# Expert lists through a table in DRAM, and bias products with 128 rows, in a mixture-of-experts layer

## The chip, the cores and the metric

The kernel runs on one core of a Trainium2 chip. The metric is the device time of one execution in microseconds. Each kernel runs several times; the median of the runs is its time. A profile is taken of one further execution.

## The reference, cut to what matters

One layer of a diffusion backbone: a state-space branch and a windowed-attention branch, merged and normalised, and then the part that is changed here, a mixture of experts over 1024 tokens of width 1024 with 32 experts, four for each token:

```python
logits = xf @ w_router + b_router
top_v, top_i = lax.top_k(logits, 4)
gates = softmax(top_v)
# for the tokens of each expert e:
gu = xb @ w_gate_up[e] + b_gate_up[e]          # 1024 -> 2048
glu, lin = split(gu); glu = min(glu, 7); lin = clip(lin, -7, 7)
act = glu * sigmoid(1.702 * glu) * (lin + 1)
y[token] += gate * (act @ w_down[e] + b_down[e])  # 1024 -> 1024
```

The result goes through a residual and a last normalisation. All is float32.

## The kernel before

**Up to the experts.** The first part (up to about 1090 us) computes both branches, the normalisation and the router. It leaves in DRAM the modulated tokens `xm_d` and the accumulator `acc_d` (residual plus gated `b_down`). It also ranks the experts by how many tokens they have (`ranks`, line 1142) and leaves on chip `posr` (for each token and rank, the token's place in that expert's list, counted from 1, or 0), the one-hot columns `pick` of the ranks, and `info` (gate in three bfloat16 pieces, tile number, row number).

**The loop over the experts** (`moe`, line 1601). The experts are taken in `ORDER`: rank 0, 31, 1, 30, 2, 29 and so on, so one with many tokens and one with few in turn. Each rank has a fixed capacity (`CAPS`, from 256 down to 128). Those of even place in the order (ranks 0 to 14) are wide: two blocks, of 128 and of 128 down to 32 tokens; the others, and the last of even place, have one block of 128 and are called narrow. An expert is twelve steps: eight for gate and up, four for down. Each step multiplies with one weight chunk of 1 MB, loaded as two `raw` pieces of 0.5 MB by SyncE (`Weights.fetch`), split on chip into a high part by ScalarE (line 1491) and a low part by VectorE (line 1493), three steps ahead of its use. Each product is made three times (high-high, high-low, low-high; lines 1306 to 1309 for narrow experts, 1359 and 1360 for wide ones, where weights stand still and tokens stream).

**Lists.** While expert i computes, the list of expert i+2 is made. After step 2 `places` (line 1197) compares `posr` with a row of numbers, eight compares on VectorE. At step 5 `slots` multiplies these one-hots with `info`, eight small bfloat16 products per block on TensorE (line 1213) with one column per list place, and seven VectorE instructions per block (lines 1217 to 1226) turn the sums into row index `ri`, write index `wi` and gate `gt`. After step 8 `start` fetches the rows of `xm_d` by `ri` with an indirect DMA of GpSimd (line 1255). The rows are transposed on TensorE in steps 1, 6, 7 and 10 of the next expert (line 1277). After the down products the result is scaled by the gate and added into `acc_d` by an indirect DMA with accumulation (line 1442).

**Bias.** Wide experts add it on ScalarE. Narrow experts add it by a product (line 1320) of a selector `sel` of 64 rows, which `constants` makes from a tile of ones and `pick` (line 1264), with `bgu`, 64 rows that hold the high and low parts of all biases. There are four such products per narrow expert, after steps 1, 3, 5 and 7.

**Order.** In the loop the order on TensorE, VectorE and ScalarE is that of the program (`manual_schedule`); on GpSimd and SyncE a planner orders by when it expects operands to be ready. `weave` takes turns between several generators of instructions. `rest` (line 1722) treats experts that overflow their capacity; there are none in these inputs.

Of the kernel before, what the change touches and what calls it, by code (L numbers as in the profile page):

```python
# [8 lines left out]
F32 = mybir.dt.float32  # L9
F32R = mybir.dt.float32r  # L10
BF16 = mybir.dt.bfloat16
I32 = mybir.dt.int32
# [10 lines left out]
KT = 8  # L23
# [58 lines left out]
def body(tc, a, o):  # L82
    nc = tc.nc
    K = Ctx()
    es = ExitStack()
    with es:
        cst = es.enter_context(tc.tile_pool(name="cst", bufs=1))
        dram = es.enter_context(tc.tile_pool(name="dram", bufs=1, space=DRAM))
        K.ident = cst.tile([128, 128], F32, name="ident")
        nc.sync.dma_start(out=K.ident, in_=a["ident"])  # L90
        K.cols = cst.tile([128, 68], F32, name="cols")
        nc.sync.dma_start(out=K.cols, in_=a["cols"])
        K.xhat_d = dram.tile([S, D], F32, name="xhat_d")
        K.rows_d = dram.tile([4, D], F32, name="rows_d")
        K.xm_d = dram.tile([S, D], F32, name="xm_d")
        K.acc_d = dram.tile([S + 128, D], F32, name="acc_d")
        K.kv_d = dram.tile([NCTX + S, 256], F32, name="kv_d")
        K.q_d = dram.tile([S, 512], F32, name="q_d")
        K.gate_d = dram.tile([16, 128, S], F32, name="gate_d")
        K.o_d = dram.tile([4, 128, S], F32, name="o_d")  # L100
        K.ssm_d = dram.tile([8, 128, S], F32, name="ssm_d")
        K.z_d = dram.tile([S, 512], F32, name="z_d")
        K.win_d = dram.tile([4, 128, 8 * 2 * 128], F32, name="win_d")
        K.wout_d = dram.tile([4, 128, 2 * 8 * 128], F32, name="wout_d")
        K.m_d = dram.tile([4, 128, 8 * 128], F32, name="m_d")
        K.tab_d = dram.tile([64, 34], F32, name="tab_d")
        K.tabe_d = dram.tile([64, 1], I32, name="tabe_d")
        K.cst = cst
        K.dram = dram
        K.parts = {}  # L110
        K.mask = cst.tile([128, 8, 2, 32], BF16, name="mask")
        K.gts = cst.tile([128, 8, 32], F32, name="gts")
        K.b_cols = a["b_cols"]
        pre(tc, a, K, es)
        moe(tc, a, K)
        finish(tc, a, o, K)

# [954 lines left out]


CAPS = [256] * 3 + [240, 224, 208] + [192] * 4 + [160] * 5 + [128] * 17
BLOCKS = {256: (128, 128), 240: (128, 112), 224: (128, 96), 208: (128, 80), 192: (128, 64), 160: (128, 32), 128: (128,), 64: (64,)}
ORDER = [r for i in range(16) for r in (i, 31 - i)]
LIMIT = 7.0
SWIGLU = 1.702
TOP = float(np.float32(LIMIT / (1 + math.exp(-SWIGLU * LIMIT))))
# [2 lines left out]
def rank_consts(tc, a, K, tmp):  # L1082
    nc = tc.nc
    v = nc.vector
    late = K.late
    K.g2 = late.tile([128, D], F32, name="g2")
    nc.sync.dma_start(out=K.g2, in_=K.rows_d[3:4, :].to_broadcast([128, D]))
    K.route = late.tile([128, 67], F32, name="route")
# [10 lines left out]
    K.info = late.tile([128, 8, 32, 6], BF16, name="info")  # L1099
    K.iota = late.tile([128, 256], BF16, name="iota")  # L1100
    K.eid = late.tile([1, 32], I32, name="eid")
    K.pick = late.tile([64, 32], F32, name="pick")
    K.cnt = late.tile([64, 32], F32, name="cnt")
    K.rid = late.tile([64, 32], F32, name="rid")
    R = K.route
# [36 lines left out]
def ranks(tc, a, K):  # L1142
# [27 lines left out]
    v.tensor_scalar(K.eid, q[0:1, 0:32], -1.0, 31.0, ALU.mult, ALU.add)  # L1170
    yield
    v.tensor_copy(K.posr, p)
    v.tensor_copy(K.pick, K.pk.bitcast(F32))
    nc.scalar.activation(out=K.rid, in_=q[0:64, 0:32], func=ACTF.Copy)
    nc.scalar.activation(out=K.cnt, in_=q[0:64, 32:64], func=ACTF.Copy)

# [1 line left out]
def rank_gates(tc, K, pool):  # L1178

    nc = tc.nc  # L1180
    p = K.tp.tile([128, 512], F32, tag="tp", name="gr")[:, 0:256].rearrange("p (t e) -> p t e", t=8)
    for t in range(8):
        nc.tensor.matmul(p[:, t], lhsT=K.gT[:, t, :], rhs=K.pick[0:32], start=True, stop=True)
    gr = pool.tile([128, 8, 32], F32, bufs=1, name="gr")
    v = nc.vector
    v.tensor_copy(gr, p)
    for j in range(3):
        v.tensor_copy(K.info[:, :, :, j], gr)
        if j < 2:
            v.tensor_tensor(gr, gr, K.info[:, :, :, j], ALU.subtract)  # L1190
# [36 lines left out]
        yield out  # L1227


TURN = 5, 9  # L1230


class Expert:
# [24 lines left out]
    def constants(self):  # L1258
        nc, P, K = self.nc, self.P, self.K
        if self.wide:  # L1260
            nc.vector.tensor_scalar(self.bias[:, 8:16], self.bias[:, 8:16], 1.0, None, ALU.add)
        else:
            s = P.pk.tile([64, 256], F32R, tag="pk", name="pk")
            nc.vector.tensor_scalar(s, K.full, self.pick, None, ALU.mult)
            self.sel = s[:, 0:128] if self.n == 128 else s[:, 128:256]

    def lo(self, b):

# [63 lines left out]
    def act(self, q):  # L1332


        nc, P, nb = self.nc, self.P, self.n
        x = self.whole(self.gu, nb, ("hg", "hu")[q])[0:nb]
        t = P.tmp.tile([128, 512], F32, tag=("sg", "um")[q], name="t")[0:nb]
        if q == 0:
            nc.scalar.activation(out=t, in_=x, func=ACTF.Sigmoid, scale=SWIGLU)
# [244 lines left out]

def expert_consts(tc, a, K, late):
    nc = tc.nc
    K.bgu = late.tile([64, 2 * D], F32R, name="bgu")
    K.full = late.tile([64, 256], F32, name="full")
    nc.gpsimd.memset(K.full, 1.0)
    nc.gpsimd.memset(K.full[:, 192:256], 0.0)  # L1590
    br = K.wp.tile([128, KT, 256], F32, tag="raw", name="br").rearrange("p k n -> p (k n)")[0:64]
    for j in range(2):
        nc.sync.dma_start(out=br[j * 32:(j + 1) * 32], in_=a["b_gate_up"])
    nc.gpsimd.tensor_scalar(br[:, D:], br[:, D:], 1.0, 1.0, ALU.add, ALU.mult)
    for c in range(4):
        b, r = (x[:, c * 512:(c + 1) * 512] for x in (K.bgu, br))
        nc.scalar.activation(out=b, in_=r, func=ACTF.Copy)
        nc.gpsimd.tensor_tensor(b[32:64], r[32:64], b[32:64].bitcast(F32), ALU.subtract)


def moe(tc, a, K):
    nc = tc.nc
    es = ExitStack()
    with es:
# [4 lines left out]
        with ExitStack() as st:  # L1609
# [10 lines left out]
                return regs[r]  # L1620

            def place(i):
                if i < len(ORDER):
                    r = ORDER[i]
                    return places(tc, K, P.li, lambda t: K.posr[:, t, r:r + 1], CAPS[r])

            def lists(i, o, *steps):
                if i < len(ORDER):
                    r = ORDER[i]
                    return slots(tc, K, P.li, K.lg, o, lambda t: K.info[:, t, r, :], BLOCKS[CAPS[r]], *steps)  # L1630

            def start(i, ls):
                if i >= len(ORDER):
# [7 lines left out]
            with tc.manual_schedule(engines={mybir.EngineType.PE, mybir.EngineType.DVE, mybir.EngineType.Activation}):  # L1641
# [14 lines left out]
                weave(W.prepare())  # L1656
                cur.constants()
            prev = None
            with tc.manual_schedule(engines={mybir.EngineType.PE, mybir.EngineType.DVE, mybir.EngineType.Activation}):
                for i in range(len(ORDER)):  # L1660
                    xs = iter(nxt.x_parts()) if nxt else iter(())
                    for c in range(12):
# [1 line left out]
                            ls = next(lists(i + 2, oh) or iter(()), None)  # L1664
                        x = next(xs, None) if c in (1, 6, 7, 10) else None
                        cur.before(c)
                        weave(prev.store(1) if c == 0 and prev else None, cur.after(c), W.prepare(), x)
                        if c == 2:
                            oh = place(i + 2)
                        if c == 8:  # L1670
# [51 lines left out]
def rest(tc, a, K):  # L1722
    nc = tc.nc
    v = nc.vector
    with ExitStack() as es:
# [4 lines left out]
        with tc.For_i(0, count, 1) as i:  # L1730
# [15 lines left out]
                v.reduce_sum(f, w, axis=AX.X)  # L1746
                v.tensor_copy(inf[:, :, c], f)
            v.tensor_copy(inf[:, :, 3:6], K.info[:, :, 0, 3:6])
            pk = sm.tile([64, 1], F32, tag="pk", name="pk")
            v.tensor_tensor(pk, K.route[0:64, 65:66], row[0:64, 33:34], ALU.is_equal)  # L1750
            W = Weights(tc, a, P)
            W.add(eid)
            e = Expert(tc, K, P, (128,), pk, next(slots(tc, K, P.li, K.lg, places(tc, K, P.li, lambda t: pos[:, t:t + 1], 128),
# [461 lines left out]
def host(inputs):  # L2215
# [14 lines left out]
    w["ln_rows"] = np.stack([f("ln1_g")[0], f("ln1_b")[0], f("ln_in_g"), f("ln_in_b")])  # L2230
    w["ln2"] = np.stack([f("ln2_g")[0], f("ln2_b")[0]])
    w["route"] = route_table()
    w["sink"] = f("attn_sink")[0]
    i = np.arange(128)
    w["band"] = np.concatenate([np.where(i[None] >= i[:, None], 0.0, NEG), np.where(i[None] <= i[:, None], 0.0, NEG)],
# [24 lines left out]
```

## Time and profile before

| | us |
|---|---|
| median of three runs | 2746.44 (2744.35 to 2754.49) |
| the profiled execution | 2748.94 |
| its span, first to last instruction | 2746.8 |
| TensorE busy (matmuls) | 2513.2 (91%) |
| VectorE busy | 2190.4 (80%) |
| ScalarE busy | 1471.6 (54%) |
| GpSimd busy | 273.7 (10%) |

Busy times are of one profiled execution. Matmuls are pipelined and overlap in the records, so what one costs is read from its start to the next start. In the profile PE is TensorE's products, PEld its weight loads, DVE is VectorE, ACT ScalarE, POOL GpSimd, SP SyncE. PEclk is the granted TensorE clock as a share of the full one.

### The profile page before, as it was taken

The page shows a single profiled execution, that of the slowest core. Times are in us where ns is not written, and L with a number is a line of the kernel's source. Part 1 is how long each engine was busy: PE and PEld are TensorE (multiplying, and loading weights), DVE is VectorE, ACT ScalarE, POOL GpSimd, SP SyncE. Part 2 cuts the span into 40 slices and gives each one's busy share as a digit, 9 for nine tenths or more (in the row PEclk, how much of TensorE's full clock was granted, in tenths as well). Part 3 has the DMA queues.
Part 4 walks back from the last instruction along what each step waited for, and adds up shares of the span by engine and source line. Part 5 has one row for each costly group of instructions (what it writes and reads, how often), then busy time and mean ns, then how long its engine had stood idle before and what let it go on. Part 6 is the DMA issues. An engine that isn't in the chain of part 4 may idle for free. (4 is left out here: it accounts for less than half of the span.)

```text
span 2746.8 us, 41465 instructions
## 1 busy us (share of the span) xinstructions
PE 2513.2 (91%) x14030; PEld 2113.3 (77%) x14030; DVE 2190.4 (80%) x4354; ACT 1471.6 (54%) x2394; POOL 273.7 (10%) x173
## 2 busy tenths in 40 slices
PE   6799999889989886899999999999999999999990
PEld 1598887767778775788878878888988887888770
DVE  9735797348787757787987987988989899989995
ACT  0622112657766312555665665666666666666661
POOL 3300000000000004010100100111011011101113
PEclk8799999999999876899999999999999999999995
DMA  7434623644686782797987987998998999899984
GB/s 250 163 121 145 209 92 114 181 160 156 229 303 242 278 294 97 238 287 218 299 266 239 306 271 243 308 300 252 301 305 269 288 310 306 274 298 303 311 279 146
DMA packets 400937, 662.57 MB, mean 241 GB/s; under 512 B 36976, under 2 KB 203760, under 8 KB 393616
## 3 DMA queue, kind: packets, MB, share of 16 engines
q1 hardware_dynamic: 388416, 615.83, 67.0%
q0 software_dynamic: 11872, 42.47, 6.7%
q8 instruction: 112, 1.84, 0.3%
q10 hardware_dynamic: 432, 1.57, 0.2%
q14 instruction: 105, 0.86, 0.1%
HBM read 570.63 MB, written 89.15 MB: 240 GB/s over the span
## 5 line engine op out<-in xcount | busy, mean ns | idle before, releaser
L1493 DVE TENSOR_TENSOR wl<-raw,wh 128x1024 fp32r<-128x1024 f32 x768 | 921.6, 1220 | 162.4 <-ACT wh L1491 161.4
L1491 ACT ACTIVATE wh<-raw 128x1024 fp32r<-128x1024 f32 x768 | 789.6, 1052 | 244.0 <-PE dn L1309 88.7
L1359 PE MATMUL uw<-x,wh 128*128 128x320 f32 (+5 forms) x1920 | 578.3, 365 | 0.2 <-issue 0.2
L1360 PE MATMUL uw<-x,wl 128*128 128x192 f32 (+4 forms) x1920 | 500.2, 261 | 0.0
L1359 PEld LDWEIGHTS uw<-x,wh 128*128 128x128 f32 x1920 | 363.1, 189 | 23.5 <-issue 0.3
L1360 PEld LDWEIGHTS uw<-x,wl 128*128 128x128 f32 x1920 | 368.2, 192 | 0.5
L1306 PE MATMUL dn<-wh,a 128*128 128x512 f32 (+4 forms) x752 | 298.7, 397 | 0.0
L1307 PE MATMUL dn<-wl,a 128*128 128x512 f32 (+4 forms) x752 | 293.5, 390 | 0.0
L1309 PE MATMUL dn<-wh,a 128*128 128x512 f32 (+3 forms) x608 | 238.5, 392 | 0.6 <-DVE a L1286 0.6
L1306 PE MATMUL up<-wh,x 128*128 128x512 f32 x544 | 221.8, 408 | 0.0
L1442 POOL DMA_INDIRECT acc_d<-y,wi x47 | 118.9, 2531 | 959.5 <-DVE y L1440 815.8
L1309 PE MATMUL up<-wh,x 128*128 128x512 f32 x544 | 213.0, 392 | 0.0
L1307 PE MATMUL up<-wl,x 128*128 128x512 f32 x544 | 212.3, 390 | 0.0
L1371 ACT ACTIVATE t<-uw,bias 128x160 f32<-128x160 f32 (+5 forms) x240 | 98.6, 419 | 131.8 <-PE uw L1360 130.9
L1306 PEld LDWEIGHTS dn<-wh,a 128*128 128x128 f32 (+4 forms) x752 | 135.7, 180 | 37.8 <-issue 4.1
L1307 PEld LDWEIGHTS dn<-wl,a 128*128 128x128 f32 (+4 forms) x752 | 135.8, 181 | 33.8
L1309 PEld LDWEIGHTS dn<-wh,a 128*128 128x128 f32 (+3 forms) x608 | 112.8, 186 | 28.4 <-DVE a L1286 2.7
L1306 PEld LDWEIGHTS up<-wh,x 128*128 128x128 f32 x544 | 102.3, 188 | 27.4 <-issue 8.4
L1309 PEld LDWEIGHTS up<-wh,x 128*128 128x128 f32 x544 | 102.1, 188 | 22.4
L1307 PEld LDWEIGHTS up<-wl,x 128*128 128x128 f32 x544 | 102.4, 188 | 18.8
L51 PE MATMUL mm<-whi,uh 128*128 128x256 f32 x320 | 108.4, 339 | 4.4 <-DVE r L307 4.4
L52 PE MATMUL mm<-wlo,uh 128*128 128x256 f32 x320 | 107.7, 337 | 0.0
(529 smaller groups left out, 4970.7 us busy)
## 6 DMA issues: line engine op xcount, KB each, us to landing
raw<-w_gate_up SPq DMA_DIRECT2D x512, 512.0 KB
raw<-w_down SPq DMA_DIRECT2D x256, 512.0 KB
mw<-w_mod SPq DMA_DIRECT2D x64, 256.0 KB
raw<-w_in SPq DMA_DIRECT2D x13, 1024.0 KB
whi<-wo SPq DMA_DIRECT2D x10, 1024.0 KB
wlo<-wo SPq DMA_DIRECT2D x10, 1024.0 KB
raw<-w_mod SPq DMA_DIRECT2D x8, 1024.0 KB
gate_d<-gs SPq DMA_DIRECT2D x16, 512.0 KB
```

The lines of the kernel that those rows point to most:

```text
L51: nc.tensor.matmul(out, lhsT=lsel(lh, k), rhs=rsel(rh, k), start=start and k == 0, stop=False)
L52: nc.tensor.matmul(out, lhsT=lsel(lh, k), rhs=rsel(rl, k), start=False, stop=False)
L1306: nc.tensor.matmul(ps, lhsT=h, rhs=wh[:, k], start=st, stop=False)
L1307: nc.tensor.matmul(ps, lhsT=h, rhs=wl[:, k], start=False, stop=en and nb <= 64)
L1309: nc.tensor.matmul(ps, lhsT=X[:, k0 + k, lo:lo + nb], rhs=wh[:, k], start=False, stop=en)
L1359: nc.tensor.matmul(p[:, 0:2 * n], lhsT=wh[:, k, fs], rhs=self.x[:, k, 0:2 * n], start=k == 0, stop=False)
L1360: nc.tensor.matmul(p[:, 0:m], lhsT=wl[:, k, fs], rhs=self.x[:, k, 0:m], start=False, stop=k == KT - 1)
L1371: nc.scalar.activation(out=y[i], in_=self.uw[i][:, 1], func=ACTF.Identity, bias=self.bias[:, q * 8 + j0 + i:q * 8 + j0 + i + 1])
L1442: nc.gpsimd.indirect_dma_start(out=K.acc_d, out_offset=bass.IndirectOffsetOnAxis(ap=wi[0:nb], axis=0), in_=o[0:nb], in_offset=None, bounds ...
L1491: nc.scalar.activation(out=h, in_=r, func=ACTF.Copy)
L1493: nc.vector.tensor_tensor(l, r, h, ALU.subtract)
```

## The change

The lists of experts 1 to 6 of the order are made as before. For the 26 others a table `list_d` in DRAM has 1280 places for each rank, of 16 bytes: row index, write index, gate, nothing. It is first filled from an input with the values for empty places. A generator `spread`, two steps of it with each product step from the first expert on, finds for each token its four ranks and places with VectorE, and writes the four entries of each token by 32 indirect DMAs of GpSimd, each of 128 entries. `table` reads the list of one block by a DMA of SyncE. The selector of the bias products, `bgu` and `pick` get 128 rows, the upper 64 zero.

```diff
+        K.list_d = dram.tile([32 * LIST, 4], I32, name="list_d")
...
+LIST = 1280
+FIRST = 6
...
+    nc.sync.dma_start(out=K.list_d, in_=a["lists"])
     K.g2 = late.tile([128, D], F32, name="g2")
...
-    K.pick = late.tile([64, 32], F32, name="pick")
+    K.pick = late.tile([128, 32], F32, name="pick")
+    v.memset(K.pick[64:128], 0.0)
...
+    K.gr = pool.tile([128, 8, 32], F32, bufs=1, name="gr0")
+    nc.scalar.activation(out=K.gr, in_=p, func=ACTF.Copy)
...
+def spread(tc, K, pool):
+    base, key, mx, oh = t_("lb", [32]), t_("lk", [8, 32]), t_("lx", [8, 8]), t_("lo", [4, 32])
+    idx, pay = t_("li", [8, 4], I32), t_("lp", [8, 4, 4], I32)
+    v.tensor_scalar(base, K.route[:, 0:32], float(LIST), None, ALU.mult)
+    v.memset(pay, 0)
+    yield
+    v.scalar_tensor_tensor(key, K.posr, 0.0, base.unsqueeze(1).to_broadcast([128, 8, 32]), ALU.is_gt, ALU.mult)
+    yield
+    v.tensor_tensor(key, key, K.posr, ALU.add)
+    yield
+    for t in range(8):
+        v.max(out=mx[:, t], in_=key[:, t])
+        v.tensor_scalar(pay[:, t, :, 0:2], K.route[:, 64:65].unsqueeze(2).to_broadcast([128, 4, 2]), 128.0 * t, None, ALU.add)
+        yield
+    v.tensor_scalar(idx, mx[:, :, 0:4], -1.0, None, ALU.add)
+    for t in range(8):
+        yield
+        v.tensor_tensor(oh, key[:, t].unsqueeze(1).to_broadcast([128, 4, 32]), mx[:, t, 0:4].unsqueeze(2).to_broadcast([128, 4, 32]), ALU.is_equal)
+        v.tensor_tensor(oh, oh, K.gr[:, t].unsqueeze(1).to_broadcast([128, 4, 32]), ALU.mult)
+        yield
+        v.reduce_sum(pay[:, t, :, 2].bitcast(F32), oh, axis=AX.X)
+        for j in range(4):
+            nc.gpsimd.indirect_dma_start(out=K.list_d, out_offset=bass.IndirectOffsetOnAxis(ap=idx[:, t, j:j + 1], axis=0),
+                                         in_=pay[:, t, j], in_offset=None, bounds_check=32 * LIST - 1, oob_is_err=True)
+            yield
...
-            s = P.pk.tile([64, 256], F32R, tag="pk", name="pk")
-            nc.vector.tensor_scalar(s, K.full, self.pick, None, ALU.mult)
-            self.sel = s[:, 0:128] if self.n == 128 else s[:, 128:256]
+            self.sel = P.pk.tile([128, 128], F32R, tag="pk", name="pk")
+            nc.vector.tensor_scalar(self.sel, K.full, self.pick, None, ALU.mult)
...
-    K.bgu = late.tile([64, 2 * D], F32R, name="bgu")
-    K.full = late.tile([64, 256], F32, name="full")
+    K.bgu = late.tile([128, 2 * D], F32R, name="bgu")
+    K.full = late.tile([128, 128], F32, name="full")
...
+    nc.gpsimd.memset(br[64:128], 0.0)
...
             def place(i):
-                if i < len(ORDER):
+                if i < FIRST:
...
+            def table(r):
+                out = []
+                for b, nb in enumerate(BLOCKS[CAPS[r]]):
+                    x = P.li.tile([128, 4], I32, tag="tab%d" % b, name="tab")
+                    nc.sync.dma_start(out=x[0:nb], in_=K.list_d[r * LIST + b * 128:r * LIST + b * 128 + nb])
+                    out.append((x[:, 0:1], x[:, 1:2], x[:, 2:3].bitcast(F32)))
+                yield out
...
-                    return slots(tc, K, P.li, K.lg, o, lambda t: K.info[:, t, r, :], BLOCKS[CAPS[r]], *steps)
+                    return table(r) if i >= FIRST else slots(tc, K, P.li, K.lg, o, lambda t: K.info[:, t, r, :], BLOCKS[CAPS[r]], *steps)
...
+            to_lists = spread(tc, K, P.li)
...
-                        weave(prev.store(1) if c == 0 and prev else None, cur.after(c), W.prepare(), x)
+                        weave(prev.store(1) if c == 0 and prev else None, cur.after(c), W.prepare(), x, limit(to_lists, 2))
...
+    w["lists"] = np.tile(np.stack([np.zeros(128), S + np.arange(128), np.zeros(128), np.zeros(128)], axis=1), (32 * LIST // 128, 1)).astype(np.int32)
```

## Rows read from the trace of the kernel before

**Rows 1.** Stretches: start:end, length, busy us (instructions) by engine, PEclk, DMA share, GB/s.
```profile
1150.00:2680.00 1530.00, 1523.08 (x8300) 1285.92 (x8298) 1351.22 (x2446) 977.88 (x1386) 166.12 (x90) 1.00 0.89 282
```
**Rows 2.** Waits, 1150 to 2650 us: who, for whom: total us, times, longest.
```profile
ACT wh L1491 <- PE dn L1309: 88.7, 66, 3.5
...
ACT wh L1491 <- DMA raw<-w_down: 0.4, 1, 0.4
```
**Rows 3.** Timeline of TensorE, narrow expert: start, length, line, product.
```profile
2008.08 0.39 PE L1309 MATMUL up<-wh,x 128*128 128x512 f32 x1
2008.39 0.49 PE L1320 MATMUL up<-bgu,pk 64*128 64x512 f32 x1
2008.82 0.50 PE L1306 MATMUL up<-wh,x 128*128 128x512 f32 x1
2009.15 0.39 PE L1307 MATMUL up<-wl,x 128*128 128x512 f32 x1
2009.38 0.40 PE L1309 MATMUL up<-wh,x 128*128 128x512 f32 x1
```
**Rows 4.** Timeline of TensorE, the same expert, third bias product.
```profile
2021.75 0.49 PE L1320 MATMUL up<-bgu,pk 64*128 64x512 f32 x1
2022.17 0.71 PE L1277 MATMUL tp<-ident,x 128*128 128x128 f32 x4
```
**Rows 5.** Timeline of TensorE, the same expert, list products.
```profile
2017.76 0.35 PE L1213 MATMUL sl<-info,oh 128*128 128x6 bf16 x8
2018.41 0.66 PE L1277 MATMUL tp<-ident,t 128*128 128x128 f32 x4 [0.30 <-DVE t L1345]
```
**Rows 6.** Timeline of TensorE, list products in two wide experts.
```profile
1466.10 0.71 PE L1213 MATMUL sl<-info,oh 128*128 128x6 bf16 x16
1466.67 0.46 PE L1359 MATMUL uw<-x,wh 128*128 128x480 f32 x1
...
1869.64 1.93 PE L1213 MATMUL sl<-info,oh 128*128 128x6 bf16 x16
1871.50 0.44 PE L1359 MATMUL uw<-x,wh 128*128 128x384 f32 x1
```
**Rows 7.** Timeline of VectorE, the narrow expert of rows 3.
```profile
2013.38 1.39 DVE L1197 TENSOR_SCALAR oh<-iota,posr 128x128 bf16<-128x128 bf16 x8
...
2017.67 0.69 DVE L1345 SCALAR_TENSOR_TENSOR t<-t 128x512 f32<-128x512 f32 x1
...
2020.54 0.20 DVE L1217 TENSOR_REDUCE L<-sl 128x6 f32<-128x48 f32 x1
```
**Rows 8.** Stretches: second expert (narrow), third (wide), four late ones.
```profile
1185.00:1222.00 37.00, 36.57 (x172) 28.23 (x171) 34.92 (x50) 26.10 (x31) 6.50 (x3) 1.00 0.98 308
1222.00:1292.00 70.00, 70.00 (x386) 59.95 (x385) 54.80 (x106) 38.52 (x60) 4.42 (x3) 1.00 0.77 241
...
2400.00:2600.00 200.00, 199.06 (x1135) 167.38 (x1135) 184.25 (x339) 135.11 (x197) 22.65 (x12) 1.00 0.94 303
```
**Rows 9.** Timeline of GpSimd, ahead of the loop and in the second expert.
```profile
1088.72 1.28 POOL L1255 DMA_INDIRECT x<-xm_d,ri  x1 [0.82 <-DVE f L1222]
1090.03 1.27 POOL L1580 TENSOR_TENSOR h<-h,y 128x512 f32<-128x512 f32 x1
...
1188.64 2.34 POOL L1442 DMA_INDIRECT acc_d<-y,wi  x1 [34.93 <-DVE y L1440]
1198.20 3.08 POOL L1442 DMA_INDIRECT acc_d<-y,wi  x1 [7.21 <-DVE oh L1197]
1205.97 1.08 POOL L1255 DMA_INDIRECT x<-xm_d,ri  x1 [4.69 <-PE tp L1277]
```
**Rows 10.** Timeline of TensorE, third expert, first transposes of the fourth's rows.
```profile
1230.04 0.60 PE L1277 MATMUL tp<-ident,x 128*128 128x128 f32 x4
```
**Rows 11.** Tile x (fetched rows), 1150 to 2650 us: from issue to landing.
```profile
DMA to landing us min/median/max: 4.0/5.9/8.2
```
**Rows 12.** DMA queue of SyncE: packets, MB, share of 16 engines.
```profile
q1 hardware_dynamic: 388416, 615.83, 67.0%
```

More of the change, by code (lines that the diff above doesn't have):

```diff
@@ L1074 @@
 CAPS = [256] * 3 + [240, 224, 208] + [192] * 4 + [160] * 5 + [128] * 17
-BLOCKS = {256: (128, 128), 240: (128, 112), 224: (128, 96), 208: (128, 80), 192: (128, 64), 160: (128, 32), 128: (128,), 64: (64,)}
+BLOCKS = {256: (128, 128), 240: (128, 112), 224: (128, 96), 208: (128, 80), 192: (128, 64), 160: (128, 32), 128: (128,)}
 ORDER = [r for i in range(16) for r in (i, 31 - i)]
+LIST = 1280
+FIRST = 6
 LIMIT = 7.0
@@ L1172, in ranks @@
     v.tensor_copy(K.posr, p)
-    v.tensor_copy(K.pick, K.pk.bitcast(F32))
+    v.tensor_copy(K.pick[0:64], K.pk.bitcast(F32))
     nc.scalar.activation(out=K.rid, in_=q[0:64, 0:32], func=ACTF.Copy)
@@ L1227, in slots @@
         yield out
+def spread(tc, K, pool):
+    nc = tc.nc
+    v = nc.vector
+    t_ = lambda n, w, d=F32: pool.tile([128] + w, d, bufs=1, name=n)
+    base, key, mx, oh = t_("lb", [32]), t_("lk", [8, 32]), t_("lx", [8, 8]), t_("lo", [4, 32])
[22 more added lines that the diff above has]
+            yield
 TURN = 5, 9
@@ L1335, in act @@
         nc, P, nb = self.nc, self.P, self.n
-        x = self.whole(self.gu, nb, ("hg", "hu")[q])[0:nb]
+        x = self.gu[0:nb]
         t = P.tmp.tile([128, 512], F32, tag=("sg", "um")[q], name="t")[0:nb]
@@ L1586, in expert_consts @@
     nc = tc.nc
-    K.bgu = late.tile([64, 2 * D], F32R, name="bgu")
-    K.full = late.tile([64, 256], F32, name="full")
+    K.bgu = late.tile([128, 2 * D], F32R, name="bgu")
+    K.full = late.tile([128, 128], F32, name="full")
     nc.gpsimd.memset(K.full, 1.0)
-    nc.gpsimd.memset(K.full[:, 192:256], 0.0)
-    br = K.wp.tile([128, KT, 256], F32, tag="raw", name="br").rearrange("p k n -> p (k n)")[0:64]
+    br = K.wp.tile([128, KT, 256], F32, tag="raw", name="br").rearrange("p k n -> p (k n)")
+    nc.gpsimd.memset(br[64:128], 0.0)
     for j in range(2):
         nc.sync.dma_start(out=br[j * 32:(j + 1) * 32], in_=a["b_gate_up"])
-    nc.gpsimd.tensor_scalar(br[:, D:], br[:, D:], 1.0, 1.0, ALU.add, ALU.mult)
+    nc.gpsimd.tensor_scalar(br[0:64, D:], br[0:64, D:], 1.0, 1.0, ALU.add, ALU.mult)
     for c in range(4):
@@ L1748, in rest @@
             v.tensor_copy(inf[:, :, 3:6], K.info[:, :, 0, 3:6])
-            pk = sm.tile([64, 1], F32, tag="pk", name="pk")
-            v.tensor_tensor(pk, K.route[0:64, 65:66], row[0:64, 33:34], ALU.is_equal)
+            pk = sm.tile([128, 1], F32, tag="pk", name="pk")
+            v.memset(pk[64:128], 0.0)
+            v.tensor_tensor(pk[0:64], K.route[0:64, 65:66], row[0:64, 33:34], ALU.is_equal)
             W = Weights(tc, a, P)
```

## The prediction

> **What bounds the kernel now.** The stretches by engine come first. From 1150 to 2680 us, the whole loop over the 32 experts, TensorE is busy 1523.08 of 1530.00 us at a granted clock of 1.00 (the upper level, 2.4 GHz) [rows 1]. Then the waits of that stretch: ScalarE's splits of the weights wait for products to give their buffers back, and for a weight load once, 0.4 us [rows 2]. So transfers and splits run ahead of TensorE, and a microsecond taken out of TensorE's stream there is a microsecond of the run until something else comes late. The timeline of TensorE then shows what its non-weight instructions cost, read from start to start.
>
> **Bias products: 64 rows become 128.** A narrow expert (one block of 128 tokens) has four. At the row of one, the product before it starts at 2008.08, the bias product at 2008.39, the next products at 2008.82, 2009.15 and 2009.38 [rows 3]. Products of 128 rows follow each other by 0.23 us; the three steps around the bias product take 1.07 instead of 0.69, so 0.38 us go. After the change it has the form of its neighbours (128 rows, 512 columns, the same type), and I give it their 0.23. The third of the four is followed by transposes: 0.42 to them instead of 0.23, and the same 0.31 ahead of it, so 0.27 [rows 4]. Per expert 3 x 0.38 + 0.27 = 1.41; 17 narrow experts: 24.0 us. Bounds: nothing (the gaps stay) and 26.
>
> **Lists of experts 7 to 32 no longer made by matmuls.** These are 13 narrow experts and 13 of even place (12 with two blocks, one with one).
> - Narrow: the eight small products start at 2017.76, the transposes behind them at 2018.41: 0.65 us, of which 0.30 is a wait of TensorE for VectorE's t of line 1345 [rows 5]. This wait would stay if VectorE were no earlier, but the eight compares of line 1197 stand ahead of that t on VectorE, 1.39 us without a gap [rows 7], and they go too. So the t is ready at about 2018.36 - 1.3 = 2017.0, before 2017.76, and all 0.65 goes: 13 x 0.65 = 8.5 us. If only 0.35 goes each time: 4.5.
> - Wide: with a second block of 64 columns the sixteen products take from 1869.64 to 1871.50, 1.86 us; with 96 columns 1466.10 to 1466.67, 0.57 us [rows 6]. I take the first price, rounded to 1.8, for the lists with second blocks of 64 or 32 columns (four and five), and the second for those of 112, 96 and 80: 9 x 1.8 + 3 x 0.57 = 17.9 us; the last one, of one block, at nothing.
>
> Together 24.0 + 8.5 + 17.9 = 50.4 us off TensorE.
>
> VectorE loses per narrow list the 1.39 us and seven small instructions, per wide list more; it is not what ends, but in a narrow expert it is busy 34.92 of 37.00 us [rows 8], so it has to become lighter by as much as TensorE for the gain to hold. TensorE's narrow expert shrinks by 1.41 + 0.65 = 2.1 us, VectorE's by 1.39 plus the seven, of which the first takes 0.20 [rows 7] and the others are of one column: about 1.0 (at most 1.4). That is 2.4: it holds.
>
> **What is added.**
> - The spreading of the lists, two steps of its generator per product step, so from the first expert to the middle of the third. On VectorE 21 instructions of 8 to 256 columns, and three of 128 columns for each of the eight token tiles. One costs between the 0.17 us of a compare (1.39 / 8) and the 0.69 of a 512-column instruction [rows 7]; I take 0.2, nearest to the compare: 9 us in all, 2.4 of them (four tiles) in the second expert, the narrow one of 34.92 in 37.00. The weights are three steps ahead, 3 x 12 products at 0.23 = 8 us, which covers it; without that cover it is 2.4, with the upper price 8. I take 2.
> - 32 indirect writes of 128 x 16 bytes on GpSimd. They delay no engine by themselves; what stands behind them on that queue is the fetch of the rows of the fourth expert and the scatters. The fetch starts at 1205.97 and its rows are first used at 1230.04 [rows 9, 10]; landing takes 4.0 to 8.2 us, median 5.9 [rows 11]. So there are 18 us to lose. Each write also waits for the one before, since all write one table: two scatters into acc_d stand 9.56 us apart for that reason (1188.64 to 1198.20). One write plus wait lies between 1.08 us (the issue of a fetch) and 5.9 us (the landing of 512 KB; this is 2 KB); I take 3. Whether this costs depends on the order on GpSimd. The order there is not that of the program: a fetch of line 1255 at 1088.72 stands ahead of an add of line 1580 at 1090.03 which is emitted earlier [rows 9]. A fetch that is ready therefore gets between two writes, and I count nothing.
> - 38 table reads of 2 KB at most on SyncE's queue. Behind eight weight loads of 0.5 MB at 303 GB/s [rows 8] one lands at worst 13.8 us late; a fetch held from 1205.97 by that and landing in 5.9 comes at 1225.7, before 1230.04. Nothing.
> - The first filling of the table, 0.66 MB DRAM to DRAM, on SyncE's queue ahead of the loads for the output projection: read and written once at 303 GB/s 4.3 us, beside other work; I take 2. Bounds 0 and the rival below.
> - The clearing of rows (GpSimd, 64 x 2048 values at most) and one more copy of the gates (ScalarE): ahead of the loop, where both engines wait most of the time; nothing, at most 3 us.
>
> **Sum.** The profiled execution took 2748.94 us: 2748.94 - 50.4 + 2 + 2 = 2702.5. The median of the three runs is 2746.44, 2.5 lower: 2700 us. With 4.5 for the narrow lists the gain is 46, with 26 for the bias products 52; less 1 to 8 that is 2695 to 2708 when the mechanism is right.
>
> **Rivals.**
> 1. The transfers or VectorE take part of it back. For: in narrow stretches the DMA share is 0.98 (1185 to 1222) and from 2400 to 2600 it is 0.94 on average [rows 8]; a stretch 3% shorter needs 0.97. Against: 0.77 in the wide stretch between, and a single wait of 0.4 us for a load in 1530 us [rows 2, 8]. If the narrow experts after the sixth give back half of their 2.1 us, 13 x 1.05 = 14 us: 2714; if all, 2728.
> 2. The chain of writes blocks GpSimd once. If the order there is that of the program, twelve writes stand between the second scatter (its issue ends 1201.28) and the fetch of the fourth expert. At 3 us each the fetch starts at 1237.3, lands at 1243.2, and TensorE stands 13 us: 2713. With 5.9 us each: 1272.1, 1278.0, 48 us: 2748, no change. Against: the reordering in [rows 9]. The Trainium skill, "DMA: Bandwidth & Descriptors", section "Anatomy of one DMA — SWDGE (gpsimd) path", speaks against the change here: a small transfer from GpSimd's queue costs about 2.0 us whatever its size, mostly the confirmation of the write, worst with HBM as target. With it one write plus issue would be 3.1 us and the stop an estimated 14 us; no row here shows so small a transfer.
> 3. Slower than before: the filling is cut as the table is shaped, into 40960 pieces of 16 bytes. By the queue's row a packet takes 0.670 x 16 x 2746.8 / 388416 = 0.076 us [rows 12]; with that 40960 x 0.076 / 16 = 195 us in which all later loads of SyncE's queue stand behind it, ahead of the router: 2700 + up to 195 = 2895. It decides from 46 us on, that is 0.018 us per piece. Against: both sides are contiguous, so nothing asks for pieces.
> 4. The change doesn't do what it says: the bias products keep their gaps. Then 24 us stay: 2724. Against: the neighbours in [rows 3] differ from it in nothing but the row count.
>
> **Chances.** Forecast 0.66, rival 1 0.13, rival 2 0.10, rival 3 0.05, rival 4 0.03, other slower ways 0.03. Likeliest 2700. The range 2688 to 2730 holds the forecast, rival 1, rival 4 and the cheaper half of rival 2. A measurement of this kernel can tell about 0.5% from no change, so faster means below 2732.7: 0.66 + 0.13 + 0.03 and half of rival 2, and some of the rest: 0.85; within 0.5%: 0.08; slower: 0.07.
>
> **What would show it.** After the change: starts around line 1320's product 0.23 apart; line 1213 with 304 products fewer; no wait of TensorE's transposes for line 1345's t from the sixth expert on; the loop over the experts about 48 us shorter, TensorE still over 99% busy in it; the time before 1150 within 3 us of before. It is wrong if TensorE has a gap of over 5 us in the third expert (rival 2), if ScalarE's splits wait for loads in narrow experts (rival 1), or if the loop starts later by tens of microseconds (rival 3).

## The result, and the profile after

The changed kernel is slower: 2763.91 us (median of 20 runs, 2754.81 to 2778.30) against 2749.23 for the kernel before in 20 runs beside it; ratio 1.0057, 95% interval 1.0046 to 1.0069. The forecast was 2700. The profiled execution has a span of 2761.9 us.

Lines moved: 1213 is now 1220, 1255 is 1294, 1277 is 1315, 1306 to 1309 are 1344 to 1347, 1320 is 1358, 1345 is 1383, 1442 is 1480, 1474 is 1512, 1491 is 1529, 1493 is 1531. New are 1264 (the writes into the table) and 1669 (the reads).

First the loop by stretches, as in [rows 1] (busy us of each engine, granted clock, DMA share, GB/s):

```profile
1150.00:2680.00 1530.00, 1479.27 (x7936) 1273.27 (x7935) 1283.31 (x1954) 978.19 (x1382) 199.22 (x121) 0.98 0.89 282
```

TensorE was busy 1523.08 of these 1530 us before. Now 51 us are idle, and the granted clock is 0.98 where it was 1.00. Over the whole loop, from the first gate-and-up product to the last down product, TensorE is busy 1530.93 of 1588.88 us; before it was 1560.12 of 1572.92. So its work did shrink, but it waits. The waits from 1150 to 2650 us (who, for whom: total us, times, longest) say for what, and answer to [rows 2]:

```profile
POOL list_d L1264 <- DMA list_d<-lp,li: 75.6, 24, 5.9
...
ACT wh L1529 <- DMA raw<-w_gate_up: 49.8, 47, 20.0
...
ACT wh L1529 <- DMA raw<-w_down: 46.7, 64, 2.2
...
PE tp L1315 <- DVE t L1383: 29.9, 12, 4.2
...
PE tp L1315 <- DMA x<-xm_d,ri: 13.3, 1, 13.3
```

ScalarE waited for weight loads 0.4 us in the loop before, 96.5 now. The waits of SyncE, which issues these loads, in the same stretch:

```profile
SPq L1669 <- DMA acc_d<-y,tab: 126.0, 19, 9.0
...
SPq L1669 <- DMA list_d<-lp,li: 32.7, 1, 32.7
```

Both lines are table reads: they stand until something else has landed, and the weight loads stand behind them.

Where in the loop this falls is seen by cutting it into experts, from each first gate-and-up product on TensorE to the next expert's (worked out from the starts, us; the experts are counted in the order in which they are taken; means where several are named). Each ratio is to executions of the kernel before taken beside that kernel, with medians from 2747.64 to 2749.23 us; it is taken over all executions and need not be the quotient of two medians.

| kernel | time, us | ratio to before, 95% interval | 3 | 4 | 8, 10, 12 | 14 to 22, narrow | 24, 26, 28 |
|---|---|---|---|---|---|---|---|
| before | 2749.23 | | 68.2 | 39.2 | 39.2 | 39.5 | 39.4 |
| after | 2763.91 | 1.0057 (1.0046 to 1.0069) | 82.6 | 52.1 | 36.9 | 43.6 | 39.1 |
| bias_only | 2742.23 | 0.9979 (0.9967 to 0.9990) | 68.2 | 39.0 | 38.9 | 39.1 | 39.0 |
| lists_only | 2762.00 | 1.0056 (1.0036 to 1.0076) | 82.7 | 51.2 | 38.4 | 41.7 | 38.9 |
| slow_writes | 2729.47 | 0.9932 (0.9912 to 0.9952) | 68.2 | 40.3 | 37.1 | 42.3 | 39.1 |
| many_bufs | 2734.67 | 0.9932 (0.9903 to 0.9961) | 82.2 | 58.9 | 37.3 | 37.4 | 37.3 |
| first8 | 2754.24 | 1.0028 (1.0017 to 1.0038) | 79.9 | 52.4 | 37.0 | 42.1 | 39.2 |
| act_reads | 2724.98 | 0.9906 (0.9883 to 0.9930) | 78.8 | 52.0 | 36.9 | 37.3 | 37.3 |
| slow_many | 2705.94 | 0.9840 (0.9826 to 0.9853) | 68.2 | 40.3 | 37.1 | 37.3 | 37.3 |
| slow_act | 2702.04 | 0.9831 (0.9817 to 0.9844) | 68.2 | 40.3 | 37.0 | 37.3 | 37.3 |
| slow_many64 | 2724.24 | 0.9914 (0.9899 to 0.9929) | 68.2 | 40.3 | 38.4 | 38.7 | 38.7 |

In after, the narrow experts 8 to 12 gain 2.3 us each, a little more than forecast, and the wide ones from 7 on 0.3 to 3.5. The third and fourth lose 27 together, the narrow ones 14 to 22 lose 4 each where they should have gained 2. Before the loop nothing is lost (first product at 1103.7 us, 1105.7 before).

**The third expert.** The timeline of GpSimd in after (start, length, line, operation, idle time before it and what ended it), answering to [rows 9]:

```profile
1204.85 1.57 POOL L1480 DMA_INDIRECT acc_d<-y,wi  x1 [5.18 <-DVE gt L1232]
1206.73 2.01 POOL L1264 DMA_INDIRECT list_d<-lp,li  x1 [0.30 <-issue]
1214.60 0.99 POOL L1264 DMA_INDIRECT list_d<-lp,li  x1 [5.86 <-DMA list_d<-lp,li]
1221.02 1.94 POOL L1264 DMA_INDIRECT list_d<-lp,li  x1 [5.43 <-DMA list_d<-lp,li]
1228.43 1.92 POOL L1264 DMA_INDIRECT list_d<-lp,li  x1 [5.48 <-DVE wl L1531]
1235.17 0.98 POOL L1264 DMA_INDIRECT list_d<-lp,li  x1 [4.82 <-DMA list_d<-lp,li]
1238.92 0.98 POOL L1264 DMA_INDIRECT list_d<-lp,li  x1 [2.77 <-DMA list_d<-lp,li]
1240.21 1.06 POOL L1294 DMA_INDIRECT x<-xm_d,ri  x1 [0.30 <-issue]
```

Six writes stand between the second scatter and the fetch of the fourth expert's rows, 6.4 us from one to the next ((1238.92 - 1206.73) / 5), because four of these five times the write waits for the landing of the one before, and once for VectorE. The fetch starts at 1240.21, 34 us later than before. TensorE then, where [rows 10] had a start at 1230.04 without a wait:

```profile
1245.21 1.09 PE L1315 MATMUL tp<-ident,x 128*128 128x128 f32 x4 [13.25 <-DMA x<-xm_d,ri]
```

These four transposes take 1.09 us against 0.60: from 1245.00 to 1248.00 us, right after the stop, the granted clock is 0.50 (the lower of its two levels, 1.2 GHz). TensorE's busy time in the third expert is 69.39 us, 1.22 more than before, and that is what the expert loses beyond the 13.25.

**The fourth expert.** SyncE's timeline in after:

```profile
1273.85 1.90 SPq L1512 DMA_DIRECT2D raw<-w_gate_up  x2
1308.53 1.87 SPq L1669 DMA_DIRECT2D tab<-list_d  x4
1310.65 1.03 SPq L1512 DMA_DIRECT2D raw<-w_gate_up  x2
```

The first table read was put ahead of the weight loads and stands 32.7 us, until the last write (issued at 1304.7) has landed. From 1260 to 1310 us the DMA share is 0.41. ScalarE's next split and, under it, TensorE's product behind it:

```profile
1314.71 1.06 ACT L1529 ACTIVATE wh<-raw 128x1024 fp32r<-128x1024 f32 x1 [20.03 <-DMA raw<-w_gate_up]
```

```profile
1315.82 0.50 PE L1344 MATMUL up<-wh,x 128*128 128x512 f32 x1 [3.70 <-ACT wh L1529]
```

TensorE is idle 10.0 us in this expert, 5.4 of them from 1330 to 1340 us, where it waits for VectorE, which is busy 19.8 us from 1320 to 1340. The granted clock over the expert is 0.90.

**The narrow experts from the fourteenth on.** SyncE and, under it, GpSimd in the sixteenth:

```profile
1915.49 10.69 SPq L1512 DMA_DIRECT2D raw<-w_gate_up  x5
1933.20 0.34 SPq L1669 DMA_DIRECT2D tab<-list_d  x1
1933.79 5.69 SPq L1512 DMA_DIRECT2D raw<-w_down  x8
```

```profile
1924.34 3.55 POOL L1480 DMA_INDIRECT acc_d<-y,tab  x1 [29.07 <-DVE y L1478]
1933.93 1.84 POOL L1480 DMA_INDIRECT acc_d<-y,tab  x1 [6.03 <-DVE wl L1531]
```

A table tile has four buffers. The read that fills one again waits until the scatter that used its old content as write indices has landed, and the planner has put that read ahead of eight loads of `w_down`. What TensorE makes of it in the sixteenth, and then the stretches of 1952 to 1958 us, of the whole sixteenth and of the twenty-fourth expert:

```profile
1952.69 1.09 PE L1315 MATMUL tp<-ident,t 128*128 128x128 f32 x4 [3.52 <-DVE t L1383]
```

```profile
1952.00:1958.00 6.00, 5.31 (x15) 4.38 (x16) 5.43 (x6) 2.83 (x4) 0.00 (x0) 0.50 1.10 349
1921.11:1964.74 43.63, 40.11 (x173) 32.19 (x172) 36.71 (x42) 28.59 (x33) 7.70 (x4) 0.92 0.95 292
2310.26:2349.17 38.91, 37.48 (x174) 30.20 (x173) 36.20 (x42) 28.54 (x33) 8.37 (x4) 1.00 0.92 288
```

TensorE stands 3.52 us, because VectorE, which makes the low parts from the splits, is late, and then runs at a granted clock of 0.50 for some microseconds. In each of the narrow experts 14 to 22 it is idle 3.0 to 4.2 us, the clock over the expert is 0.92, and its busy time is 2.7 to 2.9 us longer than in slow_act (below), where the clock is 1.00. In 24, 26 and 28 it is idle 1.4 to 2.0 us and the clock stays at 1.00. SyncE stands about as long in both groups, 6.8 to 7.7 us in each expert. So nearly half of what the experts 14 to 22 lose is slower products and not waiting.

Two rules of the Trainium skill bear on this, both on the page "DMA: Bandwidth & Descriptors", section "Anatomy of one DMA — SWDGE (gpsimd) path". It says that a wait for a semaphore is served by the engine that issues the DMA, ahead of the issue, and not by the DMA engines. The trace agrees: the waits stand on SyncE (126.0 and 32.7 us) and on GpSimd (75.6 us), and issues behind them are late. The Trainium skill also gives, in the same section, about 2.0 us for a small transfer, mostly until the write is confirmed. From issue to landing the writes of 2 KB take, by the view of the table's tile in after:

```profile
DMA to landing us min/median/max: 2.1/4.3/7.6
```

The minimum is near the figure of the Trainium skill, and the median, with weight loads running beside the writes, is twice it; the measurement decides.

### The profile page after: what moved, and what is told of

Same layout as the page of the kernel before. It is cut to its first block, busy times and chain, and to the rows that moved or that the text cites. A ratio compares the mean times of both kernels' runs of the same rounds, so it can differ in the third digit from the quotient of the medians.

```text
span 2761.9 us, 40561 instructions
## 1 busy us (share of the span) xinstructions
PE 2480.9 (90%) x13726; PEld 2109.9 (76%) x13726; DVE 2137.9 (77%) x3926; ACT 1476.5 (53%) x2395; POOL 309.2 (11%) x205
## 3 DMA queue, kind: packets, MB, share of 16 engines
q1 hardware_dynamic: 393088, 616.55, 66.5%
## 5 line engine op out<-in xcount | busy, mean ns | idle before, releaser
L1531 DVE TENSOR_TENSOR wl<-raw,wh 128x1024 fp32r<-128x1024 f32 x768 | 924.5, 1220 | 239.1 <-ACT wh L1529 234.9
L1529 ACT ACTIVATE wh<-raw 128x1024 fp32r<-128x1024 f32 x768 | 795.1, 1053 | 311.3 <-PE dn L1347 78.8
L1480 POOL DMA_INDIRECT acc_d<-y,tab x38 | 88.1, 2319 | 598.6 <-DVE y L1478 488.8
L1294 POOL DMA_INDIRECT x<-xm_d,tab x38 | 51.0, 1343 | 549.2 <-PE tp L1315 500.9
```

Source lines behind the costliest of these rows:

```text
L1294: nc.gpsimd.indirect_dma_start(out=x[0:nb], out_offset=None, in_=K.xm_d, bounds_check=S - 1, oob_is_err=True, in_offset=bass.IndirectOffse ...
L1480: nc.gpsimd.indirect_dma_start(out=K.acc_d, out_offset=bass.IndirectOffsetOnAxis(ap=wi[0:nb], axis=0), in_=o[0:nb], in_offset=None, bounds ...
L1529: nc.scalar.activation(out=h, in_=r, func=ACTF.Copy)
L1531: nc.vector.tensor_tensor(l, r, h, ALU.subtract)
```

## The experiments

**bias_only and lists_only: the two halves of the change.** bias_only is the kernel before with the 128-row parts of the diff alone. lists_only is after with

```diff
-            nc.tensor.matmul(p, lhsT=self.sel, rhs=K.bgu[:, c0:c0 + 512], start=False, stop=True)
+            nc.tensor.matmul(p, lhsT=self.sel[0:64], rhs=K.bgu[0:64, c0:c0 + 512], start=False, stop=True)
```

Expected of bias_only:

> Theory (the bias products are worth what the rows of before say, 1.41 us in each of 17 narrow experts, and the loss of the change lies in the lists alone): the kernel before with the 128-row bias products takes 24 us less than before, about 2725 us; each narrow expert shortens from 39.4 to about 38.0 us, the wide ones stay within 0.3. Rival A (the shorter narrow experts of after come from the lists that are no longer made, and the gap around the bias product is not worth 0.38): under 8 us less, 2741 or more. Rival B (shorter narrow experts run into the transfers by themselves, which is what lengthened the experts 14 to 22 of after): from the fourteenth expert on the narrow ones do not shorten, ScalarE's splits wait for loads, and the total gains at most 10 us.

Measured: 2742.23, 6.8 us below before. The narrow experts up to the thirtieth gain 0.0 to 0.5 us each, not 1.41; only the last two, during which no list is made any more, gain 1.3 and 1.4. The total is in rival A's range and the experts are as rival B has them, but the reason is neither's. The stretches of the eighteenth expert, in before, bias_only and slow_act (below), in this order:

```profile
2002.38:2041.83 39.45, 39.15 (x182) 30.20 (x180) 38.47 (x57) 28.16 (x33) 6.09 (x3) 1.00 1.00 318
```

```profile
1999.30:2038.47 39.17, 37.75 (x181) 30.46 (x180) 38.46 (x57) 28.15 (x33) 6.36 (x3) 1.00 1.01 316
```

```profile
1985.00:2022.35 37.35, 37.34 (x173) 30.27 (x172) 36.38 (x41) 28.46 (x33) 7.84 (x3) 1.00 1.00 318
```

The busy time of TensorE (second number) falls by 1.40 in bias_only, which is the forecast's 1.41. VectorE (fourth) is busy 38.46 of 39.17 and holds the expert. TensorE in bias_only, where [rows 5] had 0.30:

```profile
2013.86 0.35 PE L1214 MATMUL sl<-info,oh 128*128 128x6 bf16 x8
2015.32 0.66 PE L1277 MATMUL tp<-ident,t 128*128 128x128 f32 x4 [1.10 <-DVE t L1345]
```

In bias_only ScalarE waits only 0.3 us for weight loads from 1500 to 2650 us: the transfers are not what holds it.

Expected of lists_only:

> The kernel after with the bias products cut back to 64 rows (rows 0 to 63 of the same tiles). Theory (the losses are the chain of GpSimd's writes and SyncE's standing table reads, whatever the bias products take): the fourth expert's rows are late as after (third expert about 82, fourth about 52 us), the narrow experts 14 to 22 still take 43 to 45 us, and the total is 10 to 24 us above after, 2774 to 2788; not the whole 24, because a longer narrow expert hides more of SyncE's standing. Rival (the losses arise only because the bias products make the narrow experts too short for the transfers): narrow experts 14 to 22 take under 41 us, and the total is at or below after, 2764 or less.

Measured: 2762.00, where after has 2763.91: the whole gain of the 128 rows is lost in after. The third and fourth lose as in after; narrow experts 8 to 12 take 38.4, 1.5 more than in after; but 14 to 22 take 41.7 (40.2 to 44.0) against 43.6, so what the bias products give there, SyncE's standing takes, and more. The theory has the experts and misses the total; the rival has the total, and its bound of 41 us fails for two of the five. In these five experts TensorE is idle 17.5 us together in after and 11.0 in lists_only, and the granted clock, 0.92 in all five of after, is 0.96 in two and 1.00 in three of lists_only. The shorter experts wait longer, and more of their products run at the lower clock.

**slow_writes: the chain of writes stretched.** After with

```diff
-FIRST = 6
+FIRST = 8
...
-                        weave(prev.store(1) if c == 0 and prev else None, cur.after(c), W.prepare(), x, limit(to_lists, 2))
+                        weave(prev.store(1) if c == 0 and prev else None, cur.after(c), W.prepare(), x, limit(to_lists, 1))
```

> The kernel after with the writes spread over twice as many product steps (one step of the generator per product step in place of two) and the table read from the ninth expert on in place of the seventh; nothing else. Theory (the third and fourth expert lose because 32 writes stand in one unbroken chain ahead of the fetch of the fourth expert, and the first table read holds SyncE behind that chain): with twice the distance the fetch gets in between; the third expert comes back from 82.6 to 67 to 70 us and the fourth from 52.1 to 37 to 40; two lists more are made by products (2.5 us). Total 27 less 2.5 below after: 2737 to 2742. Narrow experts 14 to 22 stay at 43 to 45. Rival (the order on GpSimd does not follow the distance, or each write's landing is what holds the fetch however far apart the writes stand): the third expert keeps over 8 us of its 14, or the loss moves to the fifth and sixth; total within 8 us of after.

Measured: 2729.47, 34 below after, more than forecast; third expert 68.2, fourth 40.3. GpSimd's timeline shows three writes ahead of the fetch where after had six:

```profile
1202.96 1.61 POOL L1264 DMA_INDIRECT list_d<-lp,li  x1 [0.30 <-issue]
1211.74 1.26 POOL L1264 DMA_INDIRECT list_d<-lp,li  x1 [7.17 <-DMA list_d<-lp,li]
1218.32 1.92 POOL L1264 DMA_INDIRECT list_d<-lp,li  x1 [5.33 <-DVE wl L1531]
1220.54 1.12 POOL L1294 DMA_INDIRECT x<-xm_d,ri  x1 [0.30 <-issue]
```

A write is no cheaper here (median 5.4 us from issue to landing). What counts is how many of them the fetch stands behind. Narrow experts 14 to 22 still take 42.3.

**many_bufs: the reads' wait for the scatters.** After with

```diff
-                    x = P.li.tile([128, 4], I32, tag="tab%d" % b, name="tab")
+                    x = P.li.tile([128, 4], I32, tag="tab%d" % b, bufs=24, name="tab")
```

> The kernel after with 24 buffers in place of 4 for the tile that a table read fills, so that no read waits for the last user of its buffer, the scatter of an expert four or more back; nothing else. Theory (from the fourteenth expert on SyncE stands at table reads until that scatter has landed, and the weight loads behind them are late): the waits of SyncE for acc_d (126 us at line 1669) go, ScalarE no longer waits for the loads of w_down, the narrow experts 14 to 22 come from 43 to 45 back to about 37 and 24 to 28 from 39 to about 37; total 33 to 40 below after, 2724 to 2731; third and fourth expert stay long (82 and 52). Rival (the transfers themselves are too slow for the shorter experts, the wait of SyncE only fills time that the queues need anyway): narrow experts 14 to 22 stay over 41 us and the total within 10 us of after, with the DMA share at or over 0.98 there. Second rival (the reads, free of the buffer, are issued all together behind the writes and hold SyncE there longer): the fourth to sixth expert grow by over 5 us more.

Measured: 2734.67, 4 above the theory's range. The waits of SyncE for `acc_d` shrink from 126.0 us to one of 7.2, experts 14 to 28 are at 37.3 to 37.4, at a DMA share of 0.99 in the eighteenth; the transfers carry the shorter experts. The second rival holds as well, for the fourth expert: the reads, free of their buffers, are issued one after another behind the last write, and the fourth expert takes 58.9, 6.8 more than after.

**first8 and act_reads: are there two stops, or one?** first8 changes only FIRST from 6 to 8.

> The kernel after with table reads from the ninth expert on in place of the seventh, the pace of the writes as in after: it tells the fetch of the fourth expert's rows from the first table read. Theory (two stops: GpSimd's writes hold the fetch, which costs the third expert 14 us; SyncE's first read, standing until the last write lands, starves the splits and costs the fourth 13): the third expert stays at 82 to 83 us, the fourth comes back from 52.1 to 39 to 41; total 12 less 2.5 below after, 2753 to 2756. Rival (the fourth expert is late because of the third's late rows, not of the read): fourth stays over 48 us, total 2762 to 2767.

Measured: 2754.24, in the theory's range by luck: the gain comes mainly from the third expert (2.7 us) and the narrow ones 14 to 22 (7.7 together). The fourth expert still takes 52.4 and SyncE stands as long as in after, since the planner puts the later read just as early:

```profile
SPq L1669 <- DMA list_d<-lp,li: 32.3, 1, 32.3
```

The edit did not remove what it was to remove. act_reads takes the reads off SyncE:

```diff
-                    nc.sync.dma_start(out=x[0:nb], in_=K.list_d[r * LIST + b * 128:r * LIST + b * 128 + nb])
+                    nc.scalar.dma_start(out=x[0:nb], in_=K.list_d[r * LIST + b * 128:r * LIST + b * 128 + nb])
```

> The kernel after with the table reads issued by ScalarE in the order of the program in place of SyncE; the pace of the writes, the seventh expert as the first that reads, and 4 buffers as in after. In first8 SyncE still stood 32.3 us at its first read and the fourth expert still took 52.4 us, so moving the first reader did not part the two stops. Theory (two separate stops: the held fetch costs the third expert, SyncE's standing first read costs the fourth): SyncE has no read to stand at; the third expert stays at 80 to 83 us, the fourth comes back to 39 to 42, the narrow ones 14 to 28 take 37.4; total 2764 less 12 less 40, 2708 to 2716. Rival (the fourth expert is late because of the third's late rows): third 82, fourth 50 or more, total 2722 to 2728.

Measured: 2724.98, the rival's number. The narrow experts come back as the theory has it. The fourth stays at 52.0, but not for the rival's reason. GpSimd's timeline has the fetches of the fourth expert's rows and, in the last two lines, of the fifth's, which were at 1303.31 and 1305.99 in after:

```profile
1239.13 1.06 POOL L1294 DMA_INDIRECT x<-xm_d,ri  x1 [0.30 <-issue]
...
1316.26 1.06 POOL L1294 DMA_INDIRECT x<-xm_d,ri  x1 [0.30 <-issue]
...
1320.62 1.05 POOL L1294 DMA_INDIRECT x<-xm_d,ri  x1 [0.30 <-issue]
```

and TensorE now waits twice for fetched rows:

```profile
PE tp L1315 <- DMA x<-xm_d,ri: 20.3, 2, 10.8
```

With SyncE no longer standing, the DMA share from 1260 to 1310 us is 0.71 instead of 0.41, the chain ends later (last write at 1319.3, 1304.7 in after), and the fetch of the fifth expert's rows is held by it too. So one chain makes two stops in turn, and the second of them lies at the same place as SyncE's. What SyncE's first standing costs by itself is not settled: taking it away made room for another stop of the same length. A shorter one, 10.6 us in slow_writes, cost nothing: its sixth expert takes 38.96 us, and 38.95 in slow_act, where ScalarE issues the reads. In slow_many, with 10.8 us and the reads issued one after another, the sixth takes 40.57.

**slow_many and slow_act: both repairs.** slow_many has the edits of slow_writes and many_bufs, slow_act those of slow_writes and act_reads.

> Both repairs in one kernel: the writes over twice as many product steps with table reads from the ninth expert on, and 24 buffers for the tile of a table read. Theory (GpSimd's chain, SyncE's first read and SyncE's reads that wait for scatters are all that went wrong): the experts 1 to 13 take what they took in slow_writes (692 us) and 14 to 32 what they took in many_bufs (835), so span 1105 + 692 + 835 + 69 = 2701, time about 2703, ratio to before 0.983; narrow experts from the eighth on at 37.2 to 37.4. Rival (the gains of the two overlap, because in each of them the transfers catch up somewhere): 2715 to 2729.

> As slow_writes (half the pace of writes, table reads from the ninth expert on, 4 buffers), but the table reads are issued by ScalarE, in the order of the program, in place of SyncE. Theory (it is the weight loads queued behind a standing read on SyncE that cost, not the read itself nor the buffers): by its place in the program the read comes after the scatter that it would wait for, narrow experts 14 to 22 take about 37.5 us, total 2700 to 2708. If an issue on ScalarE costs what it takes there (35 of them, 0.05 to 1 us each), at most a few us more. Rival (the reads wait wherever they are issued, since the scatter of the buffer's last user lands late): ScalarE's splits stand behind the reads, the wait shows as ScalarE's at the read's line, and total is at slow_writes (2729) or above.

Measured: 2705.94 and 2702.04; both theories hold. Each is faster than the kernel before by 1.6 to 1.7%, and no stop of this kind is left: in slow_act ScalarE waits 19.6 us for weight loads in the loop, and TensorE, idle 15.67 us of the loop's 1527.00, is idle 7.0 of them in the first expert (7.3 before) and 8.0 in the second, fourth and sixth, where VectorE still makes lists or spreads them. ScalarE's waits from 1150 to 2650 us:

```profile
ACT wh L1529 <- DMA raw<-w_down: 11.0, 16, 1.7
...
ACT wh L1529 <- DMA raw<-w_gate_up: 8.6, 22, 1.0
```

**slow_many64: the bias products with VectorE relieved.** slow_many with the edit of lists_only.

> slow_many with the bias products of 64 rows (rows 0 to 63 of the same tiles): what the 128 rows are worth once the lists no longer load VectorE. Theory (the 1.41 us per narrow expert of the rows of before is right for TensorE, and bias_only gained only 0.4 of it because its narrow experts then wait for VectorE): narrow experts 8 to 28 take 38.5 to 38.8 us against 37.3, total 20 to 24 us above slow_many. Rival (the gap is worth only the 0.4 us that bias_only showed, 17 x 0.4 = 7): narrow experts at 37.7, total 5 to 9 us above slow_many.

Measured: 2724.24, 18.3 above slow_many. The narrow experts 8 to 28 take 38.2 to 38.8 against 36.9 to 37.4, summed over all narrow ones 19.6 us. The theory holds for the experts and misses its total by 2 us; the shortfall is in the experts 2, 4 and 6, which gain 0.5 together: there VectorE still makes lists or spreads them, as in bias_only.

## Why the prediction was wrong

**Bias products: right for TensorE.** In after they stand 0.23 apart from their neighbours, as [rows 3] let expect:

```profile
2026.07 0.40 PE L1347 MATMUL up<-wh,x 128*128 128x512 f32 x1
2026.30 0.40 PE L1358 MATMUL up<-bgu,pk 128*128 128x512 f32 x1
2026.53 0.39 PE L1344 MATMUL up<-wh,x 128*128 128x512 f32 x1
```

Worth 18 to 20 us once VectorE is lighter (24.0 forecast), 6.8 us without. The remark that VectorE has to shrink as much as TensorE was right, and bias_only shows what it is worth; what I left out is that the first experts don't have that relief.

**Lists: right.** A narrow expert with 64-row bias products, the eighteenth, goes from 39.45 to 38.75 us by the lists alone (slow_many64): 0.70, against 0.65 in the sum. The wide experts from the seventh on lose 19.9 us from before to slow_act; 17.9 was forecast.

**Spreading, filling, clearing: right in the main.** The first, second and fourth expert, in which VectorE makes the spread, take 0.5, 1.1 and 1.1 us more than before in slow_act. In after, at the pace of the forecast, the first two take 1.3 and 2.4 more, where 2 was forecast and 8 was the upper price. The loop starts no later. Rival 3 (pieces of 16 bytes) is false: SyncE's queue moves 393088 packets, 4672 more than in [rows 12], not 40960.

**The writes: the step that failed first.** "A fetch that is ready therefore gets between two writes, and I count nothing." The order on GpSimd is not that of the program, but it is fixed before the run, and a write that waits holds all that is behind it. One row of a fetch ahead of an add in [rows 9] did not show how many writes the planner would put ahead of the fetch. The size failed too: 3 us taken, 4.75 over the whole chain ((1304.7 - 1157.4) / 31), 6.4 where it counted; within the bounds of 1.08 and 5.9 in the mean, beyond them there. Rival 2 named this stop and, with twelve writes of 3 us in place of six of 6.4, its length to the quarter of a microsecond, by luck, since both factors were off; it had 13 us of the loss and stood at 0.10. The two scatters of [rows 9] were taken as a wait for the write before, but by the row VectorE ended that wait (7.21 <-DVE oh). That writes to one tensor wait for one another holds all the same: 24 waits, 75.6 us, in after.

**The reads: the larger failure.** "38 table reads [...] lands at worst 13.8 us late [...] Nothing." That asks when the list arrives, and the lists were in time: no product of the loop waited for rows fetched by a list from the table. It does not ask what stands behind a read that waits. For the waits on GpSimd I named the queue; for SyncE I treated the reads as transfers without a wait, though the read waits for the writes of the table and for the last user of its buffer. The wait for the writes falls into the fourth expert; the wait for scatters makes 37 us in the narrow experts 14 to 28, against slow_act 6.3 in each of five and 1.8 in each of three. many_bufs and act_reads take that part away by two different means.

**The transfers.** Rival 1 saw that narrow experts need a DMA share near 1. That is true, 1.00 at 318 GB/s in slow_act's eighteenth expert, and it is enough. ScalarE's splits did wait for loads in narrow experts, the sign named for rival 1, but because the engine that issues the loads stood: in after the eighteenth expert shows a share of 0.94 and 290 GB/s. SyncE stands 6.8 to 7.2 us in each of the narrow experts 14 to 22 and they lose 5.9 to 7.0 us each, by TensorE's wait and by the lower clock behind it; the wide experts between them, with SyncE standing up to 9.0 us, lose nothing.

**The sum.** Without the two stops it is the forecast: 2702.04 in slow_act against 2700, in part because errors cancel (the bias products gave 4 to 6 us less, the wide lists 2 more). After lies 62 above slow_act: 26 in the third and fourth expert, 37 in the narrow ones from 14 on, 1 in the second, less 2 in the sixth, where slow_act still makes a list for the eighth by products. Of these 62 us 42 are idle time of TensorE (57.95 us in the loop against 15.67), and 20 are longer busy time (1530.93 against 1511.33). Nearly all of the 20 lie in the third, the fourth and the narrow experts 14 to 22, where the granted clock is 0.90 to 0.92; the prediction has no term for products that run at a lower clock after a wait. Its chance for "faster", 0.85, is also a little less than its own terms add up to (0.66 + 0.13 + 0.03 + 0.05 = 0.87).

## What to carry to other kernels

For every DMA that is added, ask not only when it lands but what it waits for, and list what stands behind it on the engine that issues it; the reuse of its own buffer is one of these waits. A chain of dependent small writes is priced by the count ahead of the next urgent issue times the time from one write to the next under load (6.4 us here), not by bytes. A wait of TensorE can cost more than its length, because products behind it may run at the lower clock: 20 of 62 us here. When one engine is 99% busy, look at the second: a saving on TensorE alone was worth a quarter of its forecast until VectorE was relieved.

## What was not expected of the hardware

Indirect writes of 2 KB took longer the more the weight loads ran beside them: a median of 4.3 us from issue to landing in after, 4.6 in act_reads, 5.4 in slow_writes and 5.5 in slow_act, with DMA shares over the chain of 0.64, 0.75, 0.87 and 0.88. No run changes the load alone, so the cause is not shown. A second fact: in the narrow experts 14 to 22 of after, TensorE's granted clock was 0.50 for some microseconds behind waits of 3.0 to 4.2 us, and the products that ran at it cost each expert 2.7 to 2.9 us. A third was forecast, from [rows 3], and held: four products with 64 rows among products with 128 cost an expert 1.40 us more than four of 128 (38.75 and 37.35 us in the eighteenth): filling the other 64 rows with zeros is faster than leaving them out.
